# Two-block network on one Trainium2 core: gates folded into weights, norms at stage ends shared out, tiles placed on a common offset

## Chip, cores and metric

The kernel runs on one core of a Trainium2 chip (trn2). The time is the device time of one execution in microseconds; the number given is the median of several runs.

## What is computed

Two blocks in sequence, on one sequence of 512 tokens with 1024 channels, all in float32.

- The **first block** has two layers of a mixer (a short convolution, differential attention and a compressed/selected/windowed attention, joined by gates and multiplied by `w_o`), a layer norm, an FFN with a depthwise convolution (width 2816) and another layer norm.
- The **second block** has an even layer (Fourier mixing and window attention) and an odd layer (neighbourhood attention), each with a SwiGLU FFN of width 2816. A context of 256 tokens goes beside the sequence: it has a mixer output and an FFN in the even layer only. What the change touches is this:

```python
x = x + g1 * o                       # o = cat(...) @ w_out
h = _rms(x, norm2_g[i]) * (1.0 + sc2) + sh2
x = x + g2 * _swiglu(h, ffn_w_gate[i], ffn_w_up[i], ffn_w_down[i])
```

`g1`, `g2` (and `cg1`, `cg2` for the context) are vectors over the 1024 output channels, the same for all tokens; they are computed on the chip from `c_2`, `c_ctx_2` and `ada_w_2`.

## The kernel before

Tokens stand in four blocks of 128 rows (the context in two). Each product is made of three TensorE matmuls (`mm3`, L188): both operands are split into a high part, rounded to float32r, and a low part, the rest; high x high, high x low and low x high are summed in PSUM.

**Weights.** `weight` (L145) loads 128x1024 float32 by a DMA from SP's queue into one of 4 raw buffers (`wr`), makes the high part with a ScalarE cast (L160, `wh`) and the low part with a VectorE subtraction (L161, `wl`), in 3 buffers each. With `held=True` the two parts go to R tiles and stay there (L155, L156).

**Products.** `gemm_a` (L194) gives transposed results: a weight is stationary and 512 tokens stream past it. `gemm_b` (L220) gives rows: it goes over pairs of k-tiles and within each over the token blocks, with one PSUM tile per block. The last `outer` weights are held, and the loop over blocks stands outside for them, so that the blocks finish one after the other and `done(i, ps)` is called for each. `cols` is 512: each product of 1024 columns is made in two halves (`hf`).

**Gated outputs.** `gated` (L1099) is `gemm_b` with a `done` that multiplies the finished PSUM tile by the gate (`gate_add`, L1094: a VectorE product into `gx`, L1096, and a sum into the residual `x`, L1097). It is used for the mixers' outputs (`mix_out`, L1364; `odd`, L1392, where the last pair of k-tiles has its own loop `out_end`, L1433) and for `swiglu`'s down products (L1129, in 3 parts of the width, 4 for the context). The gate's two 128x512 tiles are read by `mod` (L931).

**Stage ends.** After the last sum of a token block come its square sums on ScalarE (`rms_sum`, L941), two small GpSimd instructions (L951, L952), the scaling of both halves on VectorE (`rms_mod`, L964 and L965), eight TensorE transposes (`transposed`, L291), the affine by columns (first half: four ScalarE instructions, L306; second half: a VectorE product and sum, L308 and L309) and the split into the next stage's operand (L172, L173). `after_all` (L990) puts a block's norm behind the next block's sums. At the end of the first block there is a layer norm by rows before that (`layer_norm` with `gb`, L348 and L349).

**Order.** The order on each engine is set when the program is built: the Tile framework's scheduler goes through the instructions of all engines in source order and takes first what it holds to be ready, so that neighbours of the source can change places. Each engine then works through its list in order. The context's FFN is a generator from which the even mixer's attention takes pieces by `fill` (L128), to give TensorE work between its softmax steps; in the odd mixer it is the next group's projections and, in the last group, the output product.

**Placement.** Pools take SBUF in the order in which they are opened: constants, raw weights, split weights, the X tiles (the streams' transposed operands), and then a pool for each stage, with its F tiles (float32) and R tiles (float32r) of 128x512 and its small tiles among them, in the order of first use. A tile takes a multiple of 32 bytes per partition. The constants begin at 16512 and take 2368 bytes, so weights and X tiles start at 64 modulo 128; R tiles start at 0 modulo 128 in both first mixers, in both FFNs of the first block and in the odd mixer, at 64 in the even mixer and in the FFNs of the second block.

Of the kernel before, what the change touches and what calls it, by code (L numbers as in the profile page):

```python
# [9 lines left out]
F32 = mybir.dt.float32  # L10
F32R = mybir.dt.float32r
BF = mybir.dt.bfloat16
AF = mybir.ActivationFunctionType
# [19 lines left out]
WSPLIT = 3  # L33
OUTER = 4
HEAD = 3
BG = (0.85, -6.0)
DF = (1.3, 4.0, 1.3, 1.0)
NF = (1.6, 1.2, 1.2)
# [15 lines left out]
class Gen:  # L54
    def __init__(self, ctx, tc, t):
        self.nc, self.tc, self.t = tc.nc, tc, t
        p = lambda n, b, **k: ctx.enter_context(tc.tile_pool(name=n, bufs=b, **k))
        self.cp = p("consts", 1)
        self.wp = p("wraw", WRAW)
        self.hp = p("wsplit", WSPLIT)  # L60
        self.pp = p("psum", 4, space=bass.MemoryType.PSUM)
        self.dp = p("scratch", 1, space=bass.MemoryType.DRAM)
        self.fq, self.budget, self.todo = [], 0.0, None
        self.bg, self.credit, self.rate = None, 0.0, 0.0
        nc = self.nc
        self.ident = self.const("ident")
        self.mhalf = self.cp.tile([128, 1], F32, name="mhalf", tag="mhalf")
        nc.vector.memset(self.mhalf, -0.5)
        self.ones = self.cp.tile([128, 1], F32, name="ones", tag="ones")
        nc.vector.memset(self.ones, 1.0)  # L70

    def phase(self, ctx, name, **bufs):
        self.bufs, self.pending = bufs, {}
        self.ph = ctx.enter_context(self.tc.tile_pool(name=name, bufs=1))
        self.lows, self.turn = {}, {}

    def tile(self, tag, name, shape, dt=F32):
        return self.ph.tile(list(shape), dt, name=name, tag=tag, bufs=self.bufs[tag])

    def F(self, name, n=512):  # L80
        return self.tile("F", name, [128, 512])[:, :n]
# [60 lines left out]
            self.drain(self.fq.pop(0))  # L142


    def weight(self, src, shape, held=False):  # L145

        nc = self.nc
        n = int(np.prod(shape[1:]))
        r = self.wp.tile([128, 1024], F32, name="wr", tag="wr")[:, :n]
        self.load(r, src)  # L150
        if held:
            c = shape[2]
            h, l = ([self.R("w" + a, c) for _ in range(shape[1])] for a in "hl")
            for k in range(shape[1]):
                nc.scalar.copy(h[k], r[:, k * c:k * c + c])  # L155
                nc.vector.tensor_sub(l[k], r[:, k * c:k * c + c], raw(h[k]))  # L156
            return h, l
        h = self.hp.tile([128, 1024], F32R, name="wh", tag="wh")[:, :n]
        l = self.hp.tile([128, 1024], F32R, name="wl", tag="wl")[:, :n]
        nc.scalar.copy(h, r)  # L160
        nc.vector.tensor_sub(l, r, raw(h))  # L161
        if self.bg is not None:
            self.credit += self.rate
            while self.credit >= 1.0:
                self.credit -= 1.0
                next(self.bg, None)
        return tuple(a.rearrange("p (a b) -> p a b", b=shape[2]) for a in (h, l))
# [49 lines left out]
        for src in srcs[hd:]:  # L217
            yield self.get(self.gemm_a(src, op, kt, n))

    def gemm_b(self, srcs, cols, op, nt, done, outer=1, tag="G", head=0, there=None):  # L220


        kt = sum(n for _, n in srcs)
# [17 lines left out]
        for c, (src, n) in enumerate(srcs):  # L241
            if c < head:
                continue
            keep = c >= len(srcs) - outer
            h, l = self.weight(src, (128, n, cols), outer > 1 and keep)
            if keep:
                held.append((h, l, k0, n))
            else:
                for kk in range(n):
                    for i in range(nt):  # L250
                        step(i, k0 + kk, h[:, kk], l[:, kk])
                        yield 0.00127 * cols
            k0 += n
# [37 lines left out]
    def transposed(self, xn, st, i, perm=False, ab=None):  # L291
# [3 lines left out]
        for hf in range(2):  # L295
# [4 lines left out]
            if ab is not None:  # L300
                a, b = (v[:, hf * 4:hf * 4 + 4] for v in ab)
                t = self.F("xa")
                t3 = t.rearrange("p (q t) -> p q t", q=4)
                if hf == 0:
                    for q in range(4):
                        nc.scalar.activation(t3[:, q], src[:, q], AF.Identity, scale=a[:, q:q + 1], bias=b[:, q:q + 1])  # L306
                else:
                    nc.vector.tensor_mul(t3, src, a[:, :, None].to_broadcast([128, 4, 128]))  # L308
                    nc.vector.tensor_add(t3, t3, b[:, :, None].to_broadcast([128, 4, 128]))  # L309
                src = t3  # L310
            hi, lo = st.slot(0, hf), st.slot(1, hf)
            if perm:
# [26 lines left out]
    def layer_norm(self, x, st, gb=None):  # L339
# [4 lines left out]
        rs = self.small("rstd", [128, 2])  # L344
        self.rsqrt(rs[:, 0:1], mv[:, 1:2], 1.0, LN_EPS)
        if gb is not None:
            for hf in range(2):
                nc.vector.scalar_tensor_tensor(x[hf], x[hf], mv[:, 0:1], gb[0][hf], op0=OP.subtract, op1=OP.mult)  # L348
                nc.vector.scalar_tensor_tensor(x[hf], x[hf], rs[:, 0:1], gb[1][hf], op0=OP.mult, op1=OP.add)  # L349
            return  # L350
        nc.vector.scalar_tensor_tensor(rs[:, 1:2], mv[:, 0:1], -1.0, rs[:, 0:1], op0=OP.mult, op1=OP.mult)
        for hf in range(2):
            nc.scalar.activation(x[hf], x[hf], AF.Identity, scale=rs[:, 0:1], bias=rs[:, 1:2])

# [65 lines left out]
    def low(self, n):  # L420

        if n not in self.lows:
            self.lows[n] = [self.small(f"low{n}_{i}", [128, n], F32R, bufs=1) for i in range(self.bufs["L"])]
            self.turn[n] = 0
            for t in self.lows[n]:
                self.nc.gpsimd.memset(raw(t[64:128]), 0.0)
        self.turn[n] += 1
        return self.lows[n][(self.turn[n] - 1) % self.bufs["L"]]
# [526 lines left out]
    def rms_mod(self, x, st, i, lsk, perm=False, ss=None):  # L955
# [6 lines left out]
                ss = self.rms_sum(ss, x[hf], hf)  # L962
        h = [self.F("h") for _ in range(2)]
        nc.vector.tensor_scalar(h[0], x[0], ss, None, op0=OP.mult)  # L964
        nc.vector.tensor_scalar(h[1], x[1], ss, None, op0=OP.mult)  # L965
        self.transposed(h, st, i, perm, (c[:, k * 24 + 8:k * 24 + 16], c[:, k * 24:k * 24 + 8]))

    def normed(self, z, ps, n, scale=1.0, then=None, pool=False):
# [122 lines left out]
            nc.vector.tensor_sub(o[:, g, hn:], ps[g][:, :hn], o[:, g, hn:])  # L1091
        out.extend(o[:, g] for g in range(4))

    def gate_add(self, x, ps, g):  # L1094
        t = self.F("gx")
        self.nc.vector.tensor_mul(t, ps, g)  # L1096
        self.nc.vector.tensor_add(x, x, t)  # L1097

    def gated(self, srcs, op, nt, x, hf, g, tag, outer, after):  # L1099

        nc = self.nc
# [1 line left out]
        def dn(i, ps):  # L1103
            if x[i][hf] is None:
                x[i][hf] = self.F("x")
                self.load(x[i][hf], self.xd[i, :, hf])
            self.gate_add(x[i][hf], ps, g[hf])
            if after is not None:
                after(i, hf)
        yield from self.gemm_b(srcs, 512, op, nt, dn, outer=outer, tag=tag)  # L1110
        if after is not None:
            self.after_all()

# [278 lines left out]
    def odd(self, sc, st):  # L1392
# [33 lines left out]
        def out_part():  # L1426

            g.extend(self.mod(1, 0, 2))
            for hf in range(2):
                yield from self.gated([(w[hf, c], 2) for c in range(3)], lambda k: cat[k], NT, x, hf, g, "G", 1, None)  # L1430
            ws.extend(self.weight(w[hf, 3], (128, 2, 512)) for hf in range(2))

        def out_end():  # L1433
            st.new()
            after = self.normed_after(x, st, (1, 0, 1), False, keep)
            for i in range(NT):
                for hf in range(2):
                    ps = self.P("G")
                    for kk in range(2):
# [1 line left out]
                        self.mm3(ps, cat[6 + kk][0][:, ts], cat[6 + kk][1][:, ts], ws[hf][0][:, kk], ws[hf][1][:, kk],  # L1441
                                 kk == 0, kk == 1)
                        yield 0.65
                    self.gate_add(x[i][hf], ps, g[hf])
                    after(i, hf)
            self.after_all()

# [112 lines left out]
def emit(ctx, tc, t):  # L1560
# [43 lines left out]
    with ExitStack() as cc:  # L1604
# [15 lines left out]
        with ExitStack() as c:  # L1620
# [1 line left out]
            y = rows("y", 2, t["ctx_2"])  # L1622
            g.rope2t = g.const("rope2t", pool=g.ph)
            g.wmask = g.const("wmask", BF, pool=g.ph)
            w = g.const("dftc", pool=g.ph)
            g.dftc = [g.small(f"dftc{i}", [128, 256], F32R, bufs=1) for i in range(2)]
            g.split(w, *g.dftc)
            sc = g.even(sc, sx, y)
# [180 lines left out]
```

## Time and profile before

| | us |
|---|---|
| runs (3): lowest / median / highest | 3503.96 / 3507.51 / 3509.67 |
| the profiled execution | 3504.4 |
| its span, first to last instruction | 3502.6 |
| TensorE (PE) busy | 3425.0 (98%) |
| VectorE (DVE) busy | 2185.0 (62%) |
| ScalarE (ACT) busy | 1561.5 (45%) |
| GpSimd (POOL) busy | 278.6 (8%) |

PE is TensorE's matmuls, PEld its weight loads, which run beside them. Busy time of PE is modelled: matmuls overlap, and a row's duration goes from its start to the end of its results, so the pace is read from one start to the next. Lines (L160) are those of the kernel; a helper's line stands for all who call it. In `out<-in` stand the program's names of tiles. Stages by time in us: first layer 0 to 965, second layer's mixer to 1530, its FFN to 1920, even mixer with the context's work to 2372, even FFN to 2750, odd mixer to 3136, odd FFN to the end.

### The profile page before, as it was taken

The page shows a single profiled execution, that of the slowest core. Times are in us where ns is not written, and L with a number is a line of the kernel's source. Part 1 is how long each engine was busy: PE and PEld are TensorE (multiplying, and loading weights), DVE is VectorE, ACT ScalarE, POOL GpSimd, SP SyncE. Part 2 cuts the span into 40 slices and gives each one's busy share as a digit, 9 for nine tenths or more (in the row PEclk, how much of TensorE's full clock was granted, in tenths as well). Part 3 has the DMA queues.
Part 4 walks back from the last instruction along what each step waited for, and adds up shares of the span by engine and source line. Part 5 has one row for each costly group of instructions (what it writes and reads, how often), then busy time and mean ns, then how long its engine had stood idle before and what let it go on. Part 6 is the DMA issues. An engine that isn't in the chain of part 4 may idle for free.

```text
span 3502.6 us, 48430 instructions
## 1 busy us (share of the span) xinstructions
PE 3425.0 (98%) x18702; PEld 2937.6 (84%) x18702; DVE 2185.0 (62%) x3599; ACT 1561.5 (45%) x2933; POOL 278.6 (8%) x524
## 2 busy tenths in 40 slices
PE   8999999999999999999999999999999999989999
PEld 8888888888888888888887888988888888878887
DVE  5567645999564775579857777774334566673433
ACT  5445424424364554344334567653222466652222
POOL 2200000000021000000001200000000333300000
PEclk9999999999999999999999999999999999999999
DMA  4221124675323212446743233463323322333222
GB/s 124 83 91 55 67 96 152 199 228 181 106 81 92 79 60 73 132 146 216 256 136 121 73 109 121 145 205 109 102 96 115 96 55 55 67 107 119 96 90 87
DMA packets 144646, 404.49 MB, mean 115 GB/s; under 512 B 26752, under 2 KB 35104, under 8 KB 144416
## 3 DMA queue, kind: packets, MB, share of 16 engines
q1 hardware_dynamic: 144416, 401.40, 36.1%
q8 instruction: 147, 2.41, 0.3%
q14 instruction: 83, 0.68, 0.1%
HBM read 384.46 MB, written 16.88 MB: 115 GB/s over the span
## 4 chain that ended last, share of the span: by engine, by line
PE 85%; DVE 5%; ACT 4%; issue 3%; POOL 2%; DMA 1%; SPq 0%; POOLq 0%; ACTq 0%; DVEq 0%
PE ps L190 25%; PE ps L191 25%; PE ps L192 25%; PE ps L433 1%; PE ps L434 1%; PE ps L466 1%; PE ps L776 1%; ACT stk L403 1%; PE ps L1038 1%; DVE wl L161 1%; PE ps L298 1%; PE ps L1024 1%; PE ps L685 1%; PE ps L1029 1%; POOL hrms L331 1%
## 5 line engine op out<-in xcount | busy, mean ns | idle before, releaser
L160 ACT CAST wh<-wr 128x1024 fp32r<-128x1024 f32 (+2 forms) x540 | 557.3, 1032 | 1115.4 <-PE ps L191 499.9
L161 DVE TENSOR_TENSOR wl<-wr,wh 128x1024 fp32r<-128x1024 f32 (+2 forms) x540 | 651.4, 1207 | 581.5 <-ACT wh L160 573.5
L190 PE MATMUL ps<-xq,wh 128*128 128x512 f32 (+1 forms) x2664 | 956.7, 360 | 8.5 <-ACT xq L172 6.7
L191 PE MATMUL ps<-xq,wh 128*128 128x512 f32 (+1 forms) x2664 | 945.2, 355 | 0.9 <-DVE xq L173 0.8
L192 PE MATMUL ps<-xq,wl 128*128 128x512 f32 (+1 forms) x2664 | 945.5, 355 | 0.1
L190 PEld LDWEIGHTS ps<-xq,wh 128*128 128x128 f32 x2664 | 505.9, 190 | 73.7 <-ACT xq L172 8.6
L192 PEld LDWEIGHTS ps<-xq,wl 128*128 128x128 f32 x2664 | 505.5, 190 | 69.0 <-DVE wl L161 0.3
L191 PEld LDWEIGHTS ps<-xq,wh 128*128 128x128 f32 x2664 | 505.8, 190 | 64.9 <-DVE xq L173 1.8
L190 PE MATMUL ps<-wh,xq 128*128 128x256 f32 (+3 forms) x1056 | 342.5, 325 | 2.5 <-ACT wh L160 1.3
L191 PE MATMUL ps<-wl,xq 128*128 128x256 f32 (+3 forms) x1056 | 335.1, 318 | 1.6 <-DVE wl L161 0.9
L192 PE MATMUL ps<-wh,xq 128*128 128x256 f32 (+3 forms) x1056 | 335.4, 318 | 0.7 <-DVE xq L173 0.7
L191 PE MATMUL ps<-wl,hdh 128*128 128x512 f32 x704 | 275.4, 391 | 0.0
L190 PE MATMUL ps<-wh,hdh 128*128 128x512 f32 x704 | 275.1, 391 | 0.0
L192 PE MATMUL ps<-wh,hdl 128*128 128x512 f32 x704 | 273.9, 389 | 0.0
L190 PEld LDWEIGHTS ps<-wh,xq 128*128 128x128 f32 x1056 | 202.8, 192 | 10.2 <-ACT ngate L534 1.8
L191 PEld LDWEIGHTS ps<-wl,xq 128*128 128x128 f32 x1056 | 202.5, 192 | 8.3 <-DVE wl L161 1.1
L192 PEld LDWEIGHTS ps<-wh,xq 128*128 128x128 f32 x1056 | 202.1, 191 | 7.6 <-DVE xq L173 0.9
L906 DVE SCALAR_TENSOR_TENSOR adaj<-adaw,cb 128x1024 bf16<-128x1024 f32 x160 | 194.7, 1217 | 16.5 <-DMA adaw<-in_ada_w_dram 15.8
L173 DVE TENSOR_TENSOR ptl<-ps,pth 128x512 fp32r<-128x512 f32 (+1 forms) x208 | 132.9, 653 | 52.3 <-ACT pth L172 50.7
L172 ACT CAST pth<-ps 128x512 fp32r<-128x512 f32 (+1 forms) x208 | 114.9, 573 | 94.3 <-PE ps L466 45.9
L190 PEld LDWEIGHTS ps<-wh,hdh 128*128 128x128 f32 x704 | 132.2, 188 | 28.8
L192 PEld LDWEIGHTS ps<-wh,hdl 128*128 128x128 f32 x704 | 132.1, 188 | 28.1
(438 smaller groups left out, 5302.7 us busy)
## 6 DMA issues: line engine op xcount, KB each, us to landing
wr<-in_ffn_w_gu_dram SPq DMA_DIRECT2D x132, 512.0 KB, 3.3
wr<-in_ffn_w_down_dram SPq DMA_DIRECT2D x110, 512.0 KB, 3.3
adaw<-in_ada_w_dram SPq DMA_DIRECT2D x96, 512.0 KB, 4.2
wr<-in_ffn_w_up_dram SPq DMA_DIRECT2D x88, 512.0 KB, 3.9
wr<-in_w_in_g_dram SPq DMA_DIRECT2D x48, 512.0 KB, 3.3
xd<-x SPq DMA_DIRECT2D x56, 256.0 KB, 2.0
x<-xd SPq DMA_DIRECT2D x56, 256.0 KB, 5.8
wr<-in_w_in_d_dram SPq DMA_DIRECT2D x32, 384.0 KB, 3.2
```

Source lines behind the costliest of these rows:

```text
L160: nc.scalar.copy(h, r)
L161: nc.vector.tensor_sub(l, r, raw(h))
L172: nc.scalar.copy(hi, src)
L173: nc.vector.tensor_sub(lo, src, raw(hi))
L190: mm(out, lh, rh, start=start, stop=False)
L191: mm(out, lh, rl, start=False, stop=False)
L192: mm(out, ll, rh, start=False, stop=stop)
L298: nc.tensor.transpose(ps[:, q * 128:q * 128 + 128], xn[hf][:, q * 128:q * 128 + 128], self.ident)
L331: e.tensor_tensor(out, out, self.mhalf.to_broadcast(list(out.shape)), op=OP.pow)
L403: nc.scalar.activation(dst, ps[own], AF.Copy, scale=scale[own])
L433: mm(out, q, k[0][:, ks], start=True, stop=False)
L906: nc.vector.scalar_tensor_tensor(j, w, 1.0, cb[s], op0=OP.mult, op1=OP.mult, accum_out=acc[s][:, m:m + 1])
```

## The change

`weight` gets an argument `gate`: the raw weight, once loaded, is multiplied in place by the gate's half on GpSimd, before it is split. `gemm_b` passes it on, `gated` sets it, and `gate_add` goes: the finished PSUM tile is added to the residual directly. In `transposed` the second half's affine becomes four VectorE instructions of 128x128. `rms_mod` scales the second half on GpSimd. `layer_norm` with `gb` keeps the first half on VectorE and gives the second half to ScalarE (the normalization) and GpSimd (gain and offset). A tile of 64 bytes is added to the constants, and F tiles, R tiles and the low parts of keys get a pool of their own, which is opened ahead of the stage's pool.

```diff
-    def weight(self, src, shape, held=False):
+    def weight(self, src, shape, held=False, gate=None):
...
         self.load(r, src)
+        if gate is not None:
+            r3 = r.rearrange("p (a b) -> p a b", b=shape[2])
+            nc.gpsimd.tensor_mul(r3, r3, gate[:, None, :].to_broadcast(list(shape)))
...
+        self.pad = self.cp.tile([128, PAD], F32, name="pad", tag="pad")   # PAD = 16
+        nc.gpsimd.memset(self.pad, 0.0)
...
         self.bufs, self.pending = bufs, {}
+        self.sp = ctx.enter_context(self.tc.tile_pool(name=name + "s", bufs=1))
         self.ph = ctx.enter_context(self.tc.tile_pool(name=name, bufs=1))
...
     def tile(self, tag, name, shape, dt=F32):
-        return self.ph.tile(list(shape), dt, name=name, tag=tag, bufs=self.bufs[tag])
+        return self.sp.tile(list(shape), dt, name=name, tag=tag, bufs=self.bufs[tag])
...
-                    nc.vector.tensor_mul(t3, src, a[:, :, None].to_broadcast([128, 4, 128]))
-                    nc.vector.tensor_add(t3, t3, b[:, :, None].to_broadcast([128, 4, 128]))
+                    for q in range(4):
+                        nc.vector.tensor_scalar(t3[:, q], src[:, q], a[:, q:q + 1], b[:, q:q + 1],
+                                                op0=OP.mult, op1=OP.add)
...
         if gb is not None:
-            for hf in range(2):
-                nc.vector.scalar_tensor_tensor(x[hf], x[hf], mv[:, 0:1], gb[0][hf], op0=OP.subtract, op1=OP.mult)
-                nc.vector.scalar_tensor_tensor(x[hf], x[hf], rs[:, 0:1], gb[1][hf], op0=OP.mult, op1=OP.add)
+            nc.vector.scalar_tensor_tensor(x[0], x[0], mv[:, 0:1], gb[0][0], op0=OP.subtract, op1=OP.mult)
+            nc.vector.scalar_tensor_tensor(x[0], x[0], rs[:, 0:1], gb[1][0], op0=OP.mult, op1=OP.add)
+        nc.vector.scalar_tensor_tensor(rs[:, 1:2], mv[:, 0:1], -1.0, rs[:, 0:1], op0=OP.mult, op1=OP.mult)
+        if gb is not None:
+            nc.scalar.activation(x[1], x[1], AF.Identity, scale=rs[:, 0:1], bias=rs[:, 1:2])
+            nc.gpsimd.tensor_mul(x[1], x[1], gb[0][1])
+            nc.gpsimd.tensor_add(x[1], x[1], gb[1][1])
             return
...
-        nc.vector.tensor_scalar(h[1], x[1], ss, None, op0=OP.mult)
+        nc.gpsimd.tensor_scalar(h[1], x[1], ss, None, op0=OP.mult)
...
-            self.gate_add(x[i][hf], ps, g[hf])
+            nc.vector.tensor_add(x[i][hf], x[i][hf], ps)
...
-        yield from self.gemm_b(srcs, 512, op, nt, dn, outer=outer, tag=tag)
+        yield from self.gemm_b(srcs, 512, op, nt, dn, outer=outer, tag=tag, gate=g[hf])
...
-            ws.extend(self.weight(w[hf, 3], (128, 2, 512)) for hf in range(2))
+            ws.extend(self.weight(w[hf, 3], (128, 2, 512), gate=g[hf]) for hf in range(2))
...
-                    self.gate_add(x[i][hf], ps, g[hf])
+                    nc.vector.tensor_add(x[i][hf], x[i][hf], ps)
...
-            w = g.const("dftc", pool=g.ph)
+            w = g.F("dftc", 256)
+            g.load(w, t["c_dftc"])
```

## Rows read from the trace of the kernel before

**Rows 1.** The page, part 1: busy us of each engine, share, instructions.

```profile
PE 3425.0 (98%) x18702; PEld 2937.6 (84%) x18702; DVE 2185.0 (62%) x3599; ACT 1561.5 (45%) x2933; POOL 278.6 (8%) x524
```

**Rows 2.** Stretches: us, then PE, PEld, DVE, ACT, POOL busy (x), PEclk, DMA, GB/s.

```profile
1880.00:1925.00 45.00, 38.60 (x188) 31.53 (x187) 38.84 (x65) 21.50 (x45) 9.61 (x16) 0.96 0.32 111
...
2120.00:2260.00 140.00, 139.42 (x970) 125.18 (x969) 108.07 (x199) 100.19 (x199) 2.52 (x3) 1.00 0.39 129
...
2730.00:2770.00 40.00, 33.91 (x244) 31.72 (x243) 26.07 (x56) 20.08 (x59) 17.55 (x26) 0.96 0.23 48
...
3065.00:3136.00 71.00, 58.93 (x314) 47.89 (x313) 57.97 (x102) 40.24 (x89) 5.58 (x16) 0.93 0.32 106
```

**Rows 3.** Timeline of PE, first and last of 41, 40 and 41 matmuls: start, duration.

```profile
639.72 0.39 PE L190 MATMUL ps<-xq,wh 128*128 128x512 f32 x1
...
648.79 0.39 PE L191 MATMUL ps<-xq,wh 128*128 128x512 f32 x1
...
1487.67 0.40 PE L190 MATMUL ps<-wh,mgh 128*128 128x512 f32 x1
...
1496.77 0.40 PE L190 MATMUL ps<-wh,mgh 128*128 128x512 f32 x1
...
739.65 0.39 PE L191 MATMUL ps<-wl,hdh 128*128 128x512 f32 x1
...
748.81 0.39 PE L192 MATMUL ps<-wh,hdl 128*128 128x512 f32 x1
```

**Rows 4.** Stretches of two of these, columns as in rows 2.

```profile
1488.00:1497.00 9.00, 9.00 (x40) 7.28 (x39) 7.81 (x12) 2.10 (x2) 0.00 (x0) 1.00 0.57 182
...
640.00:649.00 9.00, 9.00 (x41) 7.46 (x40) 9.00 (x15) 4.08 (x6) 0.00 (x0) 1.00 0.67 213
```

**Rows 5.** Groups of instructions: count | busy us, mean ns | idle before, releaser.

```profile
L1096 DVE TENSOR_TENSOR gx<-ps,mod 128x512 f32<-128x512 f32 x92 | 62.3, 686 | 28.3 <-PE ps L192 27.2
...
L308 DVE TENSOR_TENSOR xa<-ps,adac 128x512 f32<-128x512 f32 x22 | 15.1, 687 | 10.6 <-PE ps L298 10.5
...
L499 DVE TENSOR_SCALAR ea<-ea,nsum 128x128 f32<-128x128 f32 x32 | 9.1, 285 | 1.0
...
L982 POOL TENSOR_TENSOR z<-z,hrms 128x512 f32<-128x512 f32 x20 | 23.2, 1159 | 1.5
...
L1481 POOL TENSOR_TENSOR nam<-namask,nab 128x744 f32<-128x744 f32 x16 | 37.5, 2343 | 170.1 <-DVE onm L1494 169.1 <-DVE orc L1511 0.8
...
L353 ACT ACTIVATE x<-x,rstd 128x512 f32<-128x512 f32 x24 | 18.5, 810 | 22.6 <-DVE rstd L351 22.6
```

**Rows 6.** Timeline: a GpSimd product and a split on VectorE that meet.

```profile
2888.99 2.21 POOL L1481 TENSOR_TENSOR nam<-namask,nab 128x744 f32<-128x744 f32 x1 [30.98 <-DVE onm L1494]
...
2889.42 2.87 DVE L161 TENSOR_TENSOR wl<-wr,wh 128x1024 fp32r<-128x1024 f32 x1
```

**Rows 7.** Timeline of the odd mixer's end: start, duration [idle before <- releaser].

```profile
3119.07 0.48 DVE L964 TENSOR_SCALAR h<-x,rrs 128x512 f32<-128x512 f32 x1
...
3128.31 0.48 DVE L964 TENSOR_SCALAR h<-x,rrs 128x512 f32<-128x512 f32 x1
...
3128.93 1.94 PE L298 MATMUL ps<-ident,h 128*128 128x128 f32 x8 [7.25 <-DVE h L964]
```

**Rows 8.** Timeline of the even FFN's end.

```profile
2747.57 0.48 DVE L965 TENSOR_SCALAR h<-x,rrs 128x512 f32<-128x512 f32 x1
...
2748.19 0.63 PE L298 MATMUL ps<-ident,h 128*128 128x128 f32 x4 [2.45 <-ACT xq L172]
```

**Rows 9.** Timeline of the first block's end, last row block.

```profile
1909.59 0.55 POOL L331 TENSOR_TENSOR rstd<-rstd,mhalf 128x1 f32<-128x1 f32 x1
...
1915.81 0.74 DVE L349 SCALAR_TENSOR_TENSOR x<-x,rstd,vec 128x512 f32<-128x512 f32 x1
```

**Rows 10.** Timeline of the end: the gate's product and the last sum.

```profile
3498.32 0.69 DVE L1096 TENSOR_TENSOR gx<-ps,mod 128x512 f32<-128x512 f32 x1 [2.66 <-PE ps L192]
3499.05 0.69 DVE L1097 TENSOR_TENSOR x<-x,gx 128x512 f32<-128x512 f32 x1
```

More of the change, by code (lines that the diff above doesn't have):

```diff
@@ L35 @@
 HEAD = 3
+PAD = 16
 BG = (0.85, -6.0)
@@ L218, in gemms_a, with gemm_b @@
             yield self.get(self.gemm_a(src, op, kt, n))
-    def gemm_b(self, srcs, cols, op, nt, done, outer=1, tag="G", head=0, there=None):
+    def gemm_b(self, srcs, cols, op, nt, done, outer=1, tag="G", head=0, there=None, gate=None):
         kt = sum(n for _, n in srcs)
@@ L244, in gemm_b @@
             keep = c >= len(srcs) - outer
-            h, l = self.weight(src, (128, n, cols), outer > 1 and keep)
+            h, l = self.weight(src, (128, n, cols), outer > 1 and keep, gate)
             if keep:
@@ L346, in layer_norm @@
         if gb is not None:
-            for hf in range(2):
-                nc.vector.scalar_tensor_tensor(x[hf], x[hf], mv[:, 0:1], gb[0][hf], op0=OP.subtract, op1=OP.mult)
-                nc.vector.scalar_tensor_tensor(x[hf], x[hf], rs[:, 0:1], gb[1][hf], op0=OP.mult, op1=OP.add)
+            nc.vector.scalar_tensor_tensor(x[0], x[0], mv[:, 0:1], gb[0][0], op0=OP.subtract, op1=OP.mult)
[5 more added lines that the diff above has]
+            nc.gpsimd.tensor_add(x[1], x[1], gb[1][1])
             return
-        nc.vector.scalar_tensor_tensor(rs[:, 1:2], mv[:, 0:1], -1.0, rs[:, 0:1], op0=OP.mult, op1=OP.mult)
         for hf in range(2):
@@ L422, in low @@
         if n not in self.lows:
-            self.lows[n] = [self.small(f"low{n}_{i}", [128, n], F32R, bufs=1) for i in range(self.bufs["L"])]
+            self.lows[n] = [self.sp.tile([128, n], F32R, name=f"low{n}_{i}", tag=f"low{n}_{i}", bufs=1)
+                            for i in range(self.bufs["L"])]
             self.turn[n] = 0
@@ L1092, in fourier @@
         out.extend(o[:, g] for g in range(4))
[L1094 to L1097, printed above, removed]
     def gated(self, srcs, op, nt, x, hf, g, tag, outer, after):
```

## The prediction

> **What bounds the kernel now.** I read the page's engine shares first, then the table of stretches, then single stretches of the timeline. TensorE is busy for 98% of the span [rows 1]: what counts is how fast its matmuls follow each other and where it stands still. In the four stretches of the table [rows 2] the reader is to see two kinds of stage. Inside the second block's context work (2120 to 2260) TensorE is never free, and VectorE is busy for 108.1 of 140 us. At stage ends TensorE loses time: 6.4 of 45 us at the end of the first block, 6.1 of 40 at the end of the even layer's FFN, 12.1 of 71 at the end of the odd mixer. The granted clock there is below 1.00, at 0.93 in the last: after TensorE stood still for 7.25 us it ran a while at the lower of its two levels, 1.2 instead of 2.4 GHz [rows 2, 7]. A share of (1 - 0.93) x 71 is 5.0 us; the other two ends lose 1.8 and 1.6 us so.
>
> **Step 1: placement of tiles.** Matmuls of 512 columns don't always follow at the same pace [rows 3]. In the up product of the first FFN, 40 steps from 639.72 to 648.79 make 226.8 ns each. In the mixer's w_o, 39 steps from 1487.67 to 1496.77 make 233.3; in the first FFN's down product, 40 steps from 739.65 to 748.81 make 229.0. DMA load does not sort them: its share is 0.67 in a stretch of the fast kind and 0.57 in one of the slowest [rows 4]. Tile offsets do. Worked out from the tile sizes in order of allocation, both operands of the fast one start at 64 modulo 128 bytes, while in the slow ones the one operand starts at 64 and the other at 0. The new pad makes the constants end on a multiple of 128, and the large tiles get a pool of their own ahead of the small ones, so that all come to 0. Mismatched now are, by the loops: 2 layers x 3 branches x 8 x 4 x 3 = 576 branch products and 192 of w_o's first half, at 6.5 ns over the pace, and 2 x 432 down products of the first block and 192 of the odd layer's output, at 2.2 ns: 3.7 + 1.2 + 1.9 + 0.4 = **-7.2 us**. Ends: nothing, and -9.3 if the odd output is of the slower kind and the new common offset gains another us.
>
> **Step 2: the gates.** Removed are 92 gate multiplies on VectorE at 0.69 us [rows 5], 63 us of which nearly all lies beside TensorE's work. Added are 90 multiplies of 128x1024 on GpSimd (66 down weights, 24 output weights). No such row exists; the nearest are a plain product with a broadcast operand over 512 elements at 1.16 us and a strided one over 744 at 2.34 [rows 5], hence 2.3 to 3.2; I take 2.3, by the form that it is nearest to. That puts some 207 us on an engine that was busy for 279. A weight tile feeds 24 matmuls (5.4 us at 226.8 ns), or 12 in the context's stage, and four raw and three split buffers stand ahead of TensorE, so the 2.3 us per weight are hidden, as long as the raw buffers come free early; without that cover 90 x 2.3 = 207 us would show. Queued behind each multiply are, on GpSimd, the small rms products; on ScalarE, the cast of that weight; then VectorE's split. No DMA is added; the gate's two loads stand ahead of its weights in SP's queue as before, but are now waited for by the first weight and not by the first finished sum.
>
> **The shared wait.** Two rows show the price of a busy GpSimd: while its product ran from 2888.99 to 2891.20, a split on VectorE that started at 2889.42 took 2.87 us [rows 6]; 1.64 of that is waiting. The Trainium skill ("SBUF — State Buffer", section "SBUF: two separate sides") speaks against this change here: GpSimd and a VectorE instruction with two SBUF inputs share one port pair, held for a whole instruction, and the loser stands still. By that rule every one of the 90 multiplies can stop a split, and this row agrees with it; with all 46 named below waiting the row's 1.64 us, the sum would end at -20.6 + 75 = +55 instead of -17.6. In the FFNs of the second block VectorE has room. In the stage that is 77% busy [rows 2] it hasn't: 22 context down weights, 16 output weights there and 8 in the odd mixer make 46. If half of them meet a split, wait 0.8 us on average, and a sixth of that gets through to TensorE, it is 46 x 0.5 x 0.8 / 6 = 3 us: **+3**, between 0 and 46 x 1.64 = 75.
>
> **Step 3: stage ends.** The affine's second half now takes four VectorE pieces of 128x128 in place of a product and a sum of 0.69 each [rows 5]. A piece in SBUF takes 0.285 (the shape is there with another line); with PSUM as source I take 0.27 a step, 1.1 against 1.3 us, between 0.9 and 1.5. The norm's second half goes to GpSimd, between 0.5 (VectorE's own) and 1.16; I take 0.8, beside VectorE's 0.48.
> - Odd mixer [rows 7]: VectorE runs without a break from one norm (3119.07) to the next (3128.31), and TensorE's 7.25 us of waiting end with it. Out of these go two gate multiplies (1.2 a pair in sequence), 0.4 of the norm and 0.3 of the affine, and one multiply ahead of the first norm (0.6): -2.5. A shorter stop should give back a fifth of the clock's 5.0 us: **-3.5**. Late next: the sums themselves.
> - Even FFN [rows 8]: the last norm's second half waits until 2747.57 behind eight splits; GpSimd can start it some 2.5 us earlier. Two multiplies ahead of earlier norms give 1.4 more; with some of it lost to ScalarE's casts, **-3.5** (0 to -6).
> - First block [rows 9]: the last row block's factor is ready at 1910.1, the affine ends on VectorE at 1916.6. In its place ScalarE (0.81) and two GpSimd products (1.16 each) [rows 5] end 3.1 us after the factor; waits for the port leave perhaps 3 of the 3.4 us: **-3**, between -6 and +1.
> - The three ends without row gains save 0.2 to 0.6 each by the affine alone, and the context's and the even mixer's ends 1.5 together: **-2.7**.
> - The last sum [rows 10]: the multiply ahead of it goes, 3499.05 - 3498.32: **-0.7**, with nothing to hide it.
>
> **Sum.** -7.2 + 3 - 3.5 - 3.5 - 3 - 2.7 - 0.7 = -17.6. The profiled execution took 3504.4 us (span 3502.6 and 1.8 around it), so 3486.8; the median of the runs is 3.1 higher, so **3490**. The edits of the constant's tile (one F tile for the Fourier constant) and of the helper's order cost nothing: they run once, beside matmuls.
>
> **Rivals.**
> A. *GpSimd's port stops VectorE* in the even and odd mixers, where each weight's multiply delays the softmax work queued behind the split. For it: the 2.87 us row. Against: only a split meets it, and splits are made well ahead of their matmuls. It decides from 20.6 / 46 = 0.45 us per weight on; at 1 us it gives 3507.5 - 20.6 + 46 = 3533. Chance 0.08.
> B. *The ends don't shrink*: GpSimd's chain is as late as VectorE's was, or ScalarE's casts are late next; the ends keep their time, save the last sum. Then -7.2 - 0.7 = -7.9, with half of the port's price -6.4: 3501. For it: the port's wait [rows 6] can fall on GpSimd as well, whose products would stand between VectorE's. Against: VectorE has no gap in the odd end. Chance 0.12.
> C. *Placement does nothing*: the paces differ for another reason, and 7.2 us stay: 3497. For it: the slower ones are also other products, with other buffers. Against: the same pairs of tiles keep their pace through whole stages. Chance 0.10. The Trainium skill ("SBUF — State Buffer", section "Specifications") knows lines of 16 bytes and no larger ones; as every offset here is a multiple of 32, that rule alone makes this rival the outcome, and the three paces of the trace are not explained by it.
> The forecast has 0.70, with a range of its own from 3478 to 3500.
>
> **How the numbers follow.** About 0.2% (7 us) is what a measurement here can tell from no change. The range takes in C and most of B, and on the other side the lower ends of the stage terms: 3475 to 3505. It leaves out A and the tails. Faster: 0.68 of the forecast's 0.70, C's 0.10, a third of B: 0.82. Same: two thirds of B and the rest of the forecast: 0.10. Slower: A, 0.08.
>
> **What would show it.** Step 1: w_o and the first block's down products follow at 226.8 ns, with first and last starts as here. Step 2: GpSimd rows of 128x1024 near 2.3 us, TensorE without idle time in the second block's down products, some splits above 2 us. Step 3: TensorE's stop in the odd end at about 5 us instead of 7.25, the last norm of the even FFN before 2746 by its own clock, a granted clock at these ends nearer to 1. Wrong would be: splits of 2.5 us and more all through the even mixer with TensorE idle behind them, or paces that stay at 233.

## Result, and the profile after

The changed kernel takes **3562.4 us** (median of 4 runs, 3561.4 to 3566.3) against 3508.2 for the kernel before (4 runs): a ratio of 1.0159, 95% interval 1.0141 to 1.0176. It is 54 us slower where 17.6 less were forecast, and outside the range. The profiled execution took 3561.4 us.

Engines first (page, part 1), then the view of the core's span and mean granted clock:

```profile
PE 3440.5 (97%) x18702; PEld 2950.9 (83%) x18702; DVE 2235.1 (63%) x3549; ACT 1566.6 (44%) x2937; POOL 564.7 (16%) x645
```

```profile
core 0: 3559.6 us, clock 0.989
```

Against [rows 1], VectorE has lost 63 us of gate multiplies and yet is busy for 50 us more; GpSimd has doubled. The granted clock was 0.996 before: (1 - 0.989) x 3559.6 = 39 us of full clock are missing, 14 before. The lower of TensorE's two levels, behind its new pauses, can thus have taken at most some 25 of the 54 us; where TensorE stood still anyway, it cost nothing.

The same kinds of stretches as in [rows 2], where the stage now lies, and one more, the start of the even mixer's output:

```profile
1880.00:1925.00 45.00, 34.49 (x153) 26.68 (x151) 32.62 (x58) 21.07 (x44) 26.57 (x28) 0.94 0.25 94
2120.00:2260.00 140.00, 132.19 (x860) 114.49 (x859) 102.14 (x185) 99.88 (x206) 33.84 (x15) 0.96 0.33 110
2776.00:2816.00 40.00, 34.86 (x275) 33.31 (x274) 21.15 (x49) 19.68 (x51) 25.15 (x34) 1.00 0.37 60
3127.00:3198.00 71.00, 59.24 (x325) 48.32 (x324) 49.45 (x93) 42.21 (x96) 14.71 (x15) 0.98 0.29 100
...
2340.00:2372.00 32.00, 17.00 (x65) 12.85 (x66) 24.67 (x31) 14.34 (x29) 17.92 (x11) 0.73 0.46 153
```

TensorE, never free in the context's stretch before, now stands for 7.8 us there, and for 15 of 32 us at the start of the even output. Cut at five landmarks of TensorE's row (the last high x high matmul of each product), the two profiled executions differ so, in us:

| stretch, up to the last matmul of | before | after | |
|---|---|---|---|
| `w_o` of the second layer | 1522.1 | 1515.8 | -6.3 |
| down product of the first block | 377.3 | 390.5 | +13.2 |
| even mixer's output product | 468.3 | 506.4 | +38.1 |
| even FFN's down product | 368.7 | 366.8 | -1.9 |
| odd FFN's down product | 761.0 | 775.7 | +14.7 |

**Placement** came as forecast. Timeline of the changed kernel, first and last of 41 matmuls in `w_o` and in the first FFN's down product:

```profile
1479.67 0.39 PE L198 MATMUL ps<-wh,mgh 128*128 128x512 f32 x1
...
1488.74 0.39 PE L199 MATMUL ps<-wl,mgh 128*128 128x512 f32 x1
...
737.77 0.39 PE L198 MATMUL ps<-wh,hdh 128*128 128x512 f32 x1
...
746.84 0.39 PE L199 MATMUL ps<-wl,hdh 128*128 128x512 f32 x1
```

40 steps in 9.07 us are 226.8 ns in both, where [rows 3] had 233.3 and 229.0.

**The norm's half on GpSimd.** Timeline inside the first block's second FFN, where the context's rows are normed:

```profile
1587.98 2.92 POOL L978 TENSOR_SCALAR h<-y,rrs 128x512 f32<-128x512 f32 x1
1588.45 0.66 PE L306 MATMUL ps<-ident,h 128*128 128x128 f32 x4 [0.37 <-DVE h L977]
...
1590.95 0.66 PE L306 MATMUL ps<-ident,h 128*128 128x128 f32 x4 [1.85 <-POOL h L978]
```

The four transposes of the second half wait 1.85 us for GpSimd, whose scaling took 2.92 us; on VectorE it takes 0.48.

**The gates.** Timeline of the changed kernel at the start of the even output (SPq are DMA issues):

```profile
2343.00 0.90 SPq L126 DMA_DIRECT2D mod<-mods  x2
...
2353.05 1.82 POOL L978 TENSOR_SCALAR h<-y,rrs 128x512 f32<-128x512 f32 x1
...
2354.84 10.79 POOL L158 TENSOR_TENSOR wr<-wr,mod 128x1024 f32<-128x1024 f32 x4
...
2357.87 5.56 DVE L181 TENSOR_TENSOR xq<-xa,xq 128x512 fp32r<-128x512 f32 x2
...
2362.92 1.04 ACT L168 CAST wh<-wr 128x1024 fp32r<-128x1024 f32 x1 [1.71 <-POOL wr L158]
2363.35 5.63 DVE L169 TENSOR_TENSOR wl<-wr,wh 128x1024 fp32r<-128x1024 f32 x3
...
2366.76 0.79 PE L199 MATMUL ps<-wl,cath 128*128 128x512 f32 x1 [5.99 <-DVE wl L169]
```

Read from the bottom: TensorE waits 5.99 us for a low part; VectorE spent 5.63 us on three splits that take 1.2 each alone (the first of them 3.36), and before that 5.56 on two of 0.68; from 2354.84 to 2365.63 GpSimd ran four multiplies in a row. The gate's load went out at 2343 only, and in GpSimd's order the context's norm stood ahead of them.

The groups of the changed kernel show it over the whole span (count | busy us, mean ns | idle before, releaser):

```profile
L169 DVE TENSOR_TENSOR wl<-wr,wh 128x1024 fp32r<-128x1024 f32 x498 | 679.0, 1365 | 535.0 <-ACT wh L168 528.6 <-PE ps L462 1.8
...
L158 POOL TENSOR_TENSOR wr<-wr,mod 128x1024 f32<-128x1024 f32 x90 | 237.1, 2647 | 721.7 <-DMA wr<-in_ffn_w_down_dram 511.4 <-DMA mod<-mods 154.8 <-DMA wr<-in_ev_w_out_dram 23.5
L181 DVE TENSOR_TENSOR hdl<-sg,hdh 128x512 fp32r<-128x512 f32 x44 | 58.6, 1332 | 1.4 <-ACT hdh L180 1.4
```

### The profile page after: what moved, and what is told of

It reads as the page before. It is cut to its first block, busy times and chain, and to the rows that moved or that the text cites. A ratio compares the mean times of both kernels' runs of the same rounds, so it can differ in the third digit from the quotient of the medians.

```text
span 3559.6 us, 48688 instructions
## 1 busy us (share of the span) xinstructions
PE 3440.5 (97%) x18702; PEld 2950.9 (83%) x18702; DVE 2235.1 (63%) x3549; ACT 1566.6 (44%) x2937; POOL 564.7 (16%) x645
## 5 line engine op out<-in xcount | busy, mean ns | idle before, releaser
L169 DVE TENSOR_TENSOR wl<-wr,wh 128x1024 fp32r<-128x1024 f32 (+2 forms) x540 | 718.3, 1332 | 562.6 <-ACT wh L168 556.0
L158 POOL TENSOR_TENSOR wr<-wr,mod 128x1024 f32<-128x1024 f32 x90 | 237.1, 2647 | 721.7 <-DMA wr<-in_ffn_w_down_dram 511.4
L919 DVE SCALAR_TENSOR_TENSOR adaj<-adaw,cb 128x1024 bf16<-128x1024 f32 x160 | 194.9, 1218 | 18.8 <-DMA adaw<-in_ada_w_dram 17.9
```

What stands on the lines that cost most here:

```text
L158: nc.gpsimd.tensor_mul(r3, r3, gate[:, None, :].to_broadcast(list(shape)))
L919: nc.vector.scalar_tensor_tensor(j, w, 1.0, cb[s], op0=OP.mult, op1=OP.mult, accum_out=acc[s][:, m:m + 1])
```

## The experiments

All times are medians, each with its ratio to the kernel before on the same chip (whose medians were 3507.35, 3507.08, 3507.35 and 3505.97 us in the four groups). In the figures for stretches, "even" and "odd" are the third and the fifth row of the table above.

**1. The norm's half back on VectorE**

```diff
-        nc.gpsimd.tensor_scalar(h[1], x[1], ss, None, op0=OP.mult)
+        nc.vector.tensor_scalar(h[1], x[1], ss, None, op0=OP.mult)
```

> The changed kernel with the scaling of the norm's second half (h[1] in rms_mod) back on VectorE; all else as changed. Gate theory (the weights' multiplies on GpSimd made the loss): only what lies inside the second FFN of the first block and at its end comes back, 8 to 14 us, so 3548 to 3554 and still 1.1 to 1.3% above before. Norm theory (the 1.6 to 2.9 us scaling on GpSimd ahead of TensorE's transposes made it): most of the 54 us goes, 3515 to 3530.

Measured: 3547.1 us, 1.0111 (1.0098 to 1.0124). 15 us come back, just more than the gate theory's 8 to 14, and 7.2 of them in the first block's stretch (390.5 to 383.3). The gate theory holds; with the gates folded, the norm is 15 of the 54 us.

**2. The gates undone.** `gate_add` as before, no multiply of weights; all else as changed.

> The changed kernel with the gates back as VectorE products on the finished sums (gate_add) and plain weights; norms, affine and placement as changed. Gate theory: 36 to 45 us come back, 3517 to 3526, and the stretch from the context's down product to the odd mixer's end loses no more than before. Norm theory: less than 15 us come back, over 3547.

Measured: 3517.3 us, 1.0030 (1.0020 to 1.0040): 45 us come back, the even stretch falls from 506.4 to 471.6 and the odd one from 775.7 to 763.8. The first block's keeps its 390.6.

**3. Both undone**

> Gates and the norm's second half both back on VectorE; left of the change are placement, the four-piece affine and the layer norm split. If gates and norm are the whole loss: 3495 to 3505, below before by the placement's 6 to 7 us and a little for the affine. If the order that the scheduler makes of any edit is a cost of its own: 3510 or more.

Measured: 3508.7 us, 1.0003 (0.9994 to 1.0012): neither expectation. Gates and norm are not the whole loss; 10 us lie between this run and the next. The two also draw each other out: without folded gates the norm costs 8.5 us (run 2 to this one) and not 15.3, and without the norm the gates cost 38.4 (run 1 to this one) and not 45.2.

**4. Placement alone**

> The kernel before with the pad, the pool of its own for large tiles and the Fourier constant's tile; nothing else. Placement as predicted: 7 us below before, 3501, with w_o at 227 ns from one matmul to the next instead of 233.3 and the first block's down products at 227 instead of 229.0. Rival (the paces have another reason, or a new order eats it): 3508, within 0.1% of before.

Measured: 3498.8 us, 0.9978 (0.9969 to 0.9986), 8.5 us below before. The placement's term stands, the rival C falls.

**5. The multiply where nobody waits for it**

```diff
         nc.vector.tensor_sub(l, r, raw(h))
+        if gate is not None:
+            nc.gpsimd.tensor_mul(r, r, r)
...
```

> The third run's kernel (gates by gate_add, both halves of the norm on VectorE) with 90 GpSimd multiplies of the same size added where nobody waits for their result: each multiplies the raw weight by itself after its cast and its split, so only the raw buffer comes free later. The products are dropped, the output is that of the third run. The gates cost 38 us between the third run and the first. Port theory (a running GpSimd multiply stops VectorE, wherever it stands): 25 to 38 us of it come back as loss, 3534 to 3547. Chain theory (the multiply stands between the weight's load and its cast, and what is queued behind it waits): under 8 us, 3509 to 3517.

Measured: 3522.4 us, 1.0037 (1.0023 to 1.0052), between the two theories: 13.7 us over the third run. The even stretch is 487.9 (third run 470.9), the odd one unchanged. Each theory has a part. These multiplies took 2.05 to 2.23 us on average, where the changed kernel's took 2.65, so 13.7 may be too little for the port. From the context's first down matmul to the even output's last one (columns as in [rows 2]), the third run and this one:

```profile
2126.50:2371.00 244.50, 243.92 (x1569) 217.04 (x1568) 182.10 (x307) 152.60 (x289) 8.23 (x13) 1.00 0.49 161
```

```profile
2127.80:2386.40 258.60, 248.41 (x1568) 217.36 (x1567) 206.35 (x307) 152.62 (x289) 71.31 (x43) 0.99 0.44 152
```

VectorE has 307 instructions in both and is busy for 24.3 us longer; the stretch is 14.1 us longer.

**6. The multiply cut to one column**

```diff
-            nc.gpsimd.tensor_mul(r3, r3, gate[:, None, :].to_broadcast(list(shape)))
+            nc.gpsimd.tensor_mul(r[:, 0:1], r[:, 0:1], gate[:, 0:1])
```

> The first run's kernel (gates folded, norm on VectorE) with each weight's multiply cut to one column, 128x1 in place of 128x1024: the same waits for the gate's load, the same place in the chain, no GpSimd time and nearly no port. Left out: the gate of all other columns, so the second block's sums are not gated. Port theory and the theory that the multiply's own time makes the loss: 38 us go, 3505 to 3513. Late-gate theory (the weights wait for the gate's tile, whose load comes after the stage's other loads): at most 15 us go, 3532 to 3547.

Measured: 3529.2 us, 1.0055 (1.0038 to 1.0071): 17.9 us of the 38 go, between the two theories; 20.5 stay, with 0.25 us of GpSimd time for a weight. So a wait of its own is there, which the ninth run looks for.

**7. Placement and the four-piece affine**

> Placement and the four-piece affine, nothing else of the change. The third run (this and the split layer norm) stands 9.9 us above placement alone. If the layer norm's split on ScalarE and GpSimd makes all of that: 3498 to 3500, the affine giving at most 1 us. If the affine's pieces make a part of it (ScalarE or VectorE instructions queued in another order): 3502 to 3506.

Measured: 3503.0 us, 0.9984 (0.9976 to 0.9993), 4.2 us above placement alone, as the second expectation has it. The four pieces take 1.36 us in sequence, the product and sum that they replace 0.68 and 0.69: nothing is gained. The two intervals overlap, but the pair of runs 8 and 12, which differ in the affine alone as well, stands 4.5 apart. About half of it lies at the even FFN's end: from its last down matmul to the 192nd matmul of the next mixer's projections go 30.5 us in run 4 and 33.1 here, 28.4 in run 12 and 30.3 in run 8, and TensorE's longest wait ahead of a norm's transposes there is 3.29 us here and 2.44 in run 4. The rest is not located. The other 5.7 us up to the third run are the layer norm's.

Timeline of the third run in a row block of that layer norm:

```profile
1891.83 0.55 POOL L340 TENSOR_TENSOR rstd<-rstd,mhalf 128x1 f32<-128x1 f32 x1
...
1892.61 0.81 ACT L360 ACTIVATE x<-x,rstd 128x512 f32<-128x512 f32 x1
1893.50 1.27 POOL L361 TENSOR_TENSOR x<-x,vec 128x512 f32<-128x512 f32 x1 [1.12 <-ACT x L360]
1893.78 1.54 DVE L357 SCALAR_TENSOR_TENSOR x<-x,rstd,vec 128x512 f32<-128x512 f32 x1
...
1894.85 1.62 POOL L362 TENSOR_TENSOR x<-x,vec 128x512 f32<-128x512 f32 x1
```

From the factor (ready at 1892.38) to the second half's end 4.1 us go by, GpSimd and VectorE drawing each other out. Before, half of the work (the subtraction with the gain) stood on VectorE beside the making of the factor, and 1.4 us followed it where VectorE was free.

**8. Gates only in the two FFNs of the sequence.** Placement and affine as in run 7, `gated` folds only for `swiglu` without the context, `gate_add` elsewhere.

> Placement, the four-piece affine, and the gates folded into the weights on GpSimd only in the second block's two FFNs of the sequence (66 weights less the 22 of the context, so 44 weights), where VectorE has room; the mixers' outputs and the context keep gate_add; norms on VectorE. If folding pays where VectorE is idle: 3 to 5 us below the run without it, by the even FFN's end and the last sum, 3494 to 3497. If each GpSimd multiply costs wherever it stands: 44/90 of the 38 us, some 3517.

Measured: 3502.7 us, 0.9986 (0.9978 to 0.9995), neither expectation: no loss, and no gain over run 7. In these FFNs, where VectorE has room (busy for 143.9 of 358 us from 2372 to 2730 of the kernel before), folding is free: TensorE has no wait in this run from 2400 to 2720.

**9. Gates loaded early**

```diff
+        g1 = self.mod_own(0, 1, 2)     # two tiles of their own, loaded at the stage's start
...
-        g = self.mod(l, s, 2)
```

> The first run's kernel (3547), with the gates of the even layer's three output products (context output, context FFN, sequence output) in two tiles of their own, loaded a stage ahead, in place of two of the stage's 21 F tiles taken when the product begins. The odd mixer is left as it is. Late-gate theory (the weights' multiplies wait for the gate's load, and ScalarE's casts for them): the stretch from the first block's end to the first context down product falls from 208.5 to about 199 us, the sequence output from 91.7 to about 80, together 3525 to 3532. Rival (the multiplies' place in GpSimd's and ScalarE's order makes it, not the load): both stretches stay, 3540 or more.

Measured: 3539.4 us, 1.0092 (1.0076 to 1.0107): 7.7 us, half of what the theory asked. Between the context's first and last down matmul and the even output's last one (landmarks other than the expectation's), the even output's part came as expected (67.2 to 55.3 us) and the stage's start fell by 6.2 (238.5 to 232.3), but 6.6 us were given back in the context's FFN (201.1 to 207.7). The run also leaves the stage 19 F tiles in place of 21; what that costs was not tried apart.

**10. The odd mixer's multiplies on VectorE**

```diff
-            nc.gpsimd.tensor_mul(r3, r3, gate[:, None, :].to_broadcast(list(shape)))
+            (eng or nc.gpsimd).tensor_mul(r3, r3, gate[:, None, :].to_broadcast(list(shape)))
```

> As the ninth run, and the odd mixer's eight output weights are multiplied by their gate on VectorE in place of GpSimd. Queue theory (on GpSimd they stand behind products of the softmax that wait for VectorE, and ScalarE's exponentials stand behind their casts): the odd mixer with its output and the last FFN falls from 735 to 728 to 730 us, 5 to 7 us below the ninth run. Rival (any multiply ahead of the split delays the softmax there, VectorE's as well): no change or longer.

Measured: 3533.0 us, 1.0071 (1.0058 to 1.0085), 6.5 us below; the odd stretch falls from 772.0 to 764.3. In the first run's timeline one sees the queue: ScalarE stands 2.63 us in front of a cast with the softmax's exponentials behind it, because the multiply ran behind the mask product of the next head.

```profile
3085.53 2.17 POOL L1489 TENSOR_TENSOR nam<-namask,nab 128x744 f32<-128x744 f32 x1 [30.57 <-DVE onm L1502]
3087.68 2.34 POOL L158 TENSOR_TENSOR wr<-wr,mod 128x1024 f32<-128x1024 f32 x1
...
3090.05 1.04 ACT L168 CAST wh<-wr 128x1024 fp32r<-128x1024 f32 x1 [2.63 <-POOL wr L158]
3091.00 0.47 ACT L1512 ACTIVATE ew<-ps,onm 128x256 f32<-128x256 f32 x1
```

Run 13 has the same odd mixer and 768.3 there, so the size of this part is known to 4 us only.

**11. The norm's half as a product**

```diff
-        nc.gpsimd.tensor_scalar(h[1], x[1], ss, None, op0=OP.mult)
+        nc.gpsimd.tensor_mul(h[1], x[1], ss.to_broadcast([128, 512]))
```

> The second run's kernel (gates by gate_add, 3517) with the norm's second half on GpSimd as a product with a broadcast factor in place of a scaling by a per-partition scalar. In the trace of before such a product of 128x512 took 1.16 us, the scaling 1.58 here. If the scaling's length is the price: 3512 to 3514, a third to a half of the 8.5 us between the second and the third run. If what counts is that it runs on GpSimd at all, with VectorE at work beside it: 3516 to 3519, and the product takes 1.6 us or more.

Measured: 3512.0 us, 1.0014 (1.0005 to 1.0023), 5.2 below the second run, as the first expectation has it, though the two intervals touch. So the length is most of the price by the medians; the execution that was profiled here, 3521.4 us, lies above all the others, and its trace can't show where. Instructions of this line in this run and in the second (ns min/median/max):

```profile
L978 POOL TENSOR_TENSOR h<-x,rrs x16: 1040/1042/1319, 1893.8 to 3153.7; 128x512 f32<-128x512 f32 x16
```

```profile
L978 POOL TENSOR_SCALAR h<-x,rrs x16: 1577/1581/2924, 1893.8 to 3149.3; 128x512 f32<-128x512 f32 x16
```

**12. Placement, and gates in the FFNs.** Run 8 with the affine as before.

> The best version seen so far, placement alone (0.9978 of before), and the gates folded only in the two FFNs of the sequence; the affine as in before. If folding there pays by the even FFN's end and the last sum: 0.9968 to 0.9974 of before, 3496 to 3498. If it does not: 0.9978 again, or above.

Measured: 3498.2 us, 0.9973 (0.9963 to 0.9983). With run 4 the best version; the two are not told apart.

**13 and 14. What is left in the even layer.** Run 13 gives `nc.vector` to the even layer's products as run 10 does to the odd one's (a multiply takes 1.24 us there); run 14 is run 9 with the one-column multiply of run 6.

> As the tenth run (3533), and the even layer's 38 multiplies (context output and FFN, sequence output) are on VectorE too; GpSimd keeps the 44 of the two FFNs. If GpSimd's running time beside VectorE makes the rest of the loss: the three stretches from the first block's end to the even output's end fall from 496 us to 471 to 482, 3508 to 3519 in all, although VectorE, 77% busy there, gets 38 x 1.2 = 46 us more. If the multiply's place ahead of the cast makes it, on whichever engine: 490 us or more there, 3527 or more.

> As the ninth run (3539, gates of the even layer loaded early), with each multiply cut to one column (left out: the gate of all other columns). If GpSimd's running time makes the rest: the same three stretches fall from 495 us to 471 to 477; the odd mixer keeps its order on GpSimd and its 737 us; 3516 to 3522. If the place in the chain makes it: 488 us or more, 3531 or more.

Measured: 3512.6 us, 1.0017 (1.0007 to 1.0026), and 3511.2, 1.0015 (1.0005 to 1.0024); the even stretch, 496.4 in run 10 and 495.3 in run 9, is 475.7 and 474.8. Both meet the first expectation or better it. From the context's first down matmul to the even output's last one (columns as in [rows 2]), runs 1, 13 and 14:

```profile
2136.10:2404.40 268.30, 248.34 (x1537) 216.64 (x1538) 202.04 (x269) 150.16 (x277) 77.87 (x39) 0.96 0.45 145
```

```profile
2123.50:2372.00 248.50, 245.46 (x1582) 219.08 (x1581) 199.15 (x315) 156.28 (x296) 8.85 (x13) 1.00 0.45 154
```

```profile
2125.90:2371.90 246.00, 244.44 (x1568) 216.94 (x1567) 169.73 (x287) 153.75 (x293) 16.45 (x39) 1.00 0.46 158
```

VectorE is as busy with the multiplies (199 us) as it was with GpSimd's beside it (202), but TensorE stands still for 3.0 us in place of 20.0, and the clock stays at 1.00.

Runs 1, 6, 9 and 14 make a square: an early load gives 7.7 us under the full multiply and 18.0 under the one-column one, the short multiply 17.9 under the late load and 28.3 under the early one. With both, 2.5 us are left over the third run, which the intervals don't tell apart. So the late load and the multiply's own time are the gates' loss, and neither has a price of its own: each hides part of the other.

In run 14 the split behind the SwiGLU product shows its length without GpSimd: 684 ns, against 1332 in the changed kernel. These 44 splits stand in the two FFNs of the sequence; in run 8 they take 1230 and cost nothing. A split that waits is a loss only where TensorE waits for it.

```profile
L181 DVE TENSOR_TENSOR hdl<-sg,hdh 128x512 fp32r<-128x512 f32 x44 | 30.1, 684 | 1.4 <-ACT hdh L180 1.4
```

## Why the prediction was wrong

The runs make a staircase from the changed kernel down to the one before. Each step is the difference of two medians, good to 3 or 4 us, so that the steps of 3.9 and 4.2 are hardly clear of nothing; another order of steps would share the loss out otherwise (runs 3 and 14):

| from | to | us |
|---|---|---|
| changed, 3562.4 | run 1: norm's half on VectorE | -15.3 |
| run 1 | run 9: gates loaded early | -7.7 |
| run 9 | run 10: odd multiplies on VectorE | -6.5 |
| run 10 | run 13: even multiplies on VectorE | -20.3 |
| run 13 | run 3: no gates folded | -3.9 |
| run 3 | run 7: layer norm as before | -5.7 |
| run 7 | run 4: affine as before | -4.2 |
| run 4 | before, 3507.4 | +8.5 |

- **Step 1 (placement), -7.2: right.** Run 4 gives -8.5, and in the changed kernel `w_o` and the first block's down product both follow at 226.8 ns. Rival C, which the lines of 16 bytes in the Trainium skill ("SBUF — State Buffer", section "Specifications") would have made the outcome, is refuted; which property of the offsets counts was not tried apart. (The term's lower end, -9.3, comes to some -9.0 by its own parts; nothing hangs on it.)
- **Step 2 (the gates), "hidden": failed.** The length was taken well, 2.3 us estimated and 2.35 alone (2.65 on average, 2.3 to 3.2 were the bounds), and in the second block's FFNs the cover holds: run 8 loses nothing. What failed is the sentence that four raw and three split buffers hide the multiply "as long as the raw buffers come free early". Two things make it false elsewhere. The gate is read at the product's first weight and its load is late; that was named, and charged at nothing (7.7 us, and 18.0 where the multiply is short). And what is queued behind the multiply was listed without a price: in the odd mixer the softmax's exponentials stand behind a cast that waits for GpSimd (6.5 us).
- **The shared wait, "+3": the mis-sized term.** Its count was about right, its wait and its share were not. In the changed kernel 29 VectorE instructions beside the 46 multiplies are longer than the shortest row of their form (21 weights' splits, and most of the others splits of hidden activations and of norms), where half of 46 were expected; they lose 51 us in sum, 1.8 each and not 0.8. "A sixth of that gets through to TensorE" was chosen for splits made well ahead of their matmuls. At the start of a product there is nothing ahead, and VectorE was already 77% busy: in run 5 its 24.3 us more go with 14.1 more of the stretch, over half. In that run nobody waits for the multiplies' results, only the raw buffers come free later, and they cost 13.7 us in all. Moving the even layer's multiplies off GpSimd gave 20.3, in which the port and the shorter way from load to cast are not parted. The prediction's own sign of being wrong, long splits in the even mixer with TensorE idle behind them, is what the rows from 2357 to 2367 show.
- **Rival A had the side, and part of the mechanism**; its chance of 0.08 was far too low. All that belongs to the gates is 3547.1 - 3508.7 = 38.4 us, 0.83 for each of the 46 weights, beyond the 0.45 that rival A named as its point. But 13.7 us of port are 0.30 a weight, below it: the late load and the queues make up the rest. The Trainium skill ("SBUF — State Buffer", section "SBUF: two separate sides") says that whichever of the two instructions starts first keeps the shared port for its whole length, while the other stands still. The trace agrees: of the 44 SwiGLU splits in the changed kernel, the 13 that began while a multiply ran take 2.75 to 2.91 us, and the others 0.68 to 0.69.
- **Step 3 (stage ends), -13.4 in all: failed at the norm and the layer norm.** The scaling on GpSimd was put at 0.8 us, between 0.5 and 1.16, by the nearest products; it takes 1.58 to 2.92, outside both bounds. The form (a per-partition scalar) was the wrong one to liken to a product: run 11 has that at 1.04. At the context's norm inside the first block's FFN, to which the prediction gave no term of its own, nothing covers it. The layer norm's split, -3, costs 5.7: the last row block was read alone [rows 9], where VectorE was late; in the others the split moves work behind the factor. The affine, 1.1 for 1.3 us, takes 1.36.
- **What step 3 had right.** The last sum: from the last matmul's start to the end go 4.72 us before and 3.95 after, -0.7 predicted. The even mixer's end: the even FFN's stretch, which begins with it, falls by 1.9. The even FFN's end, in part: counted as in run 7 it falls from 32.5 to 30.3 us, but run 4, which leaves the ends alone, has 30.5; folding gives 2.1 more in run 12, and the affine takes them back in run 8. The odd end: from the output's last matmul to the last down one 377.5 us become 372.6, and 369.3 with the norm on VectorE (run 1), against 377.7 in run 3. The output's last matmul itself comes 19.6 us later than before, counted from the even FFN's last one, so part of that gain may be waiting that was done earlier. TensorE's longest wait there is 2.67 us instead of the 7.25 of [rows 7], and for GpSimd now:

```profile
3192.32 0.84 PE L306 MATMUL ps<-ident,h 128*128 128x128 f32 x4 [2.67 <-POOL h L978]
```

- **The clock** was counted as a gain at the ends. In the odd end it is one (0.93 to 0.98 in 71 us of each kernel); over the span the new pauses took up to 25 us. That is a part of the rows above and not a further one; no run moves the clock alone.

What stays open: the 3.9 us of gates with no GpSimd multiply in the mixers, half of the affine's 4 us, why the context's FFN gave back 6.6 us in run 9, and how the 20.3 us divide between the port and the way from load to cast. Every edit also has the order on the engines planned anew, and stretches that a run does not touch differ by up to 7 us between single traces (the one up to `w_o`: 1511.3 in run 7, 1518.6 in run 3).

## What to carry to other kernels

Work that moves to an idle engine is paid where it meets the busy one: cost it stage by stage, by what the loaded engine loses while the other runs, whether TensorE waits for that, and what is queued behind it in order, not by the free engine's share of the span. Fold a vector into a weight only where its load is early and the split's engine has room; at a product's first weights nothing is ahead to hide it. For an instruction that is new on an engine, a row of another form is no bound.

## What the runs showed of the hardware

- GpSimd's scaling of 128x512 by a per-partition scalar takes 1.58 us alone and up to 2.92 beside VectorE, its product with a broadcast factor 1.04, VectorE's scaling 0.48. The Trainium skill ("GPSIMD Engine Reference", section "Engine selection") puts GpSimd's one-input operations at roughly line rate; the scaling has one tensor input, takes 3.3 times VectorE's time here, and the measurement decides.
- A VectorE split of 128x512 with two inputs in SBUF takes 0.68 us, and 2.75 to 2.91 when it begins while a GpSimd multiply of 128x1024 runs (13 of 44); in the even output's start, two took 5.56.
- 512-column matmuls whose two operands start at a common offset modulo 128 bytes follow at 226.8 ns, at different ones at 229.0 or 233.3 (offsets worked out from the order of allocation).
